# A streaming prefix log-sum-exp: straight-line programs with rising semaphores in place of token loops, and a different last tile

## The chip, the cores and the metric

One core of one Trainium2 chip runs the kernel. The metric is device microseconds of one execution on that core.

## The reference

The input is 8 x 4096 x 2048 in float32 (268 MB), and so is the output. Along the middle axis each output row is the logarithm of the sum of exponentials of all rows so far:

```python
out[:, 0, :] = x[:, 0, :]
for t in range(1, S):
    mx = np.maximum(out[:, t - 1, :], x[:, t, :])
    out[:, t, :] = mx + np.log(np.exp(out[:, t - 1, :] - mx) + np.exp(x[:, t, :] - mx))
```

## The kernel before

The kernel works on 64 tiles of 4 MB: 128 partitions with 4 successive rows of 2048 columns each, so that a partition's part is 32 KB in one piece, in memory and on the chip. Six tile buffers turn round. For each tile, ScalarE takes the exponential in two column halves; VectorE sums the 4 rows of each partition (`local`); TensorE multiplies the partition totals by a triangle of ones, which gives what lies before each partition (`triangle`); VectorE adds it (`join`); TensorE carries the last partition's total to the next tile (`carry`); ScalarE takes the logarithm, and issues the store. SyncE issues the loads.

Three of the engines run loops of six tiles. So that a loop's turns can all wait for the same numbers, each wait is a token: it waits for a count and takes it off again.

```python
def take(engine, s, n):
    event(engine, [(s, n)], [(s, "sem-sub-imm", n)])
...
@block.sync                       # loads
    sp.dma_start(out=ti[0][:, 0:2, :], in_=x_v[0][:, 0:2, :]).then_inc(top, 16)
    sp.dma_start(out=ti[0][:, 2:R, :], in_=x_v[0][:, 2:R, :]).then_inc(loaded[0], 16)
    ...
    with sp.Fori(1, turns + 1) as j:
        for n in range(NI):
            take(sp, stored[n], 16)
            load(x_v[bass.ds(j * NI + n, 1)][0], n)
    ...
    for n in range(NT - NI, NT):  # last waits, inside the block
        take(sp, stored[n % NI], 32 if n >= NT - 2 else 16)
...
@block.scalar                     # its end: tiles 62 and 63 leave in column halves
    exp(n, 0)
    if n < NT - 1:
        exp(n, 1)
    ln(up, 0, turn)
    if n == NT - 1:
        store(up, o_v[up], turn, 0)
        exp(n, 1)
    ln(up, 1, turn)
    store(up, o_v[up], turn, 1 if n == NT - 1 else None)
    ...
    for h in range(2):
        ln(NT - 1, h, NT - 1 - first)
        store(NT - 1, o_v[NT - 1], NT - 1 - first, h)
    settle(NT - first)            # takes the tokens of a turn off
```

The softmax here doesn't subtract the row's maximum and nothing guards it: scores larger than these inputs give would overflow.

## Time and profile before

| | before |
|---|---|
| time, median of the first 3 runs | 1250.83 us (1250.73 to 1252.3) |
| bytes read and written | 537 MB |
| mean rate over the span | 430 GB/s |
| instructions in the record | 3456 |
| busy share of VectorE / ScalarE | 82% / 73% |

The page's DMA row says in tenths how busy the 16 DMA engines are in each of 40 slices, the row under it how much they moved. In the groups, the last column says how long the engine stood idle before such an instruction and what ended that. The prediction below shows the main lines. Two more lines of the page, the packets and the second instruction queue, are needed later:

```profile
DMA packets 20409, 537.01 MB, mean 430 GB/s; under 512 B 2096, under 2 KB 2096, under 8 KB 4144
...
q14 instruction: 2, 0.02, 0.0%
```

Packets under 8 KB are the semaphore writes (2096) and the 2048 packets of 4 KB in which the last two tiles leave. And the first transfer, in the order of time (start, duration):

```profile
1.03 0.39 SPq L114 DMA_DIRECT2D ti<-in_x_dram  x1
```

### The profile page before, as it was taken

What the parts mean: (1) busy time and instruction counts of PE and PEld (TensorE: products, weight loads), DVE (VectorE), ACT (ScalarE), POOL (GpSimd) and SP (SyncE); (2) the same over time, 40 slices, a digit from 0 to 9 for tenths busy, and PEclk for the clock granted to TensorE, in tenths of its full rate; (3) what the DMA queues carried; (4) which work ended last, traced back from release to release, by engine and by line L of the source; (5) the groups of instructions that cost most, each with busy time, mean ns of one, the idle gap of its engine ahead of it and who ended that gap; (6) DMA issues with size and microseconds to landing.
All of it is one profiled execution on the core that took longest, in us unless ns stands there. A gap on an engine that the chain in (4) does not pass through costs nothing. (4 is left out here: it accounts for less than half of the span.)

```text
span 1249.0 us, 3456 instructions
## 1 busy us (share of the span) xinstructions
PE 650.8 (52%) x960; PEld 215.3 (17%) x960; DVE 1023.0 (82%) x512; ACT 907.2 (73%) x258; POOL 1.1 (0%) x8
## 2 busy tenths in 40 slices
PE   3556455554566545655455544565545564465541
PEld 1112111111112111211111111121111121111110
DVE  4999978778787787887878878778787787877873
ACT  5897866867768677686776866867768677686774
POOL 0000000000000000000000000000000000000000
PEclk9897778786887868778778786777878878678785
DMA  9999999999999999999999999999999999999998
GB/s 403 420 436 430 433 430 437 433 431 434 430 436 434 431 433 430 437 434 430 434 430 436 436 430 434 430 436 437 428 434 431 436 436 429 434 430 436 436 430 354
DMA packets 20409, 537.01 MB, mean 430 GB/s; under 512 B 2096, under 2 KB 2096, under 8 KB 4144
## 3 DMA queue, kind: packets, MB, share of 16 engines
q1 hardware_dynamic: 9360, 268.44, 49.9%
q10 hardware_dynamic: 11040, 268.44, 49.9%
q8 instruction: 7, 0.11, 0.0%
q14 instruction: 2, 0.02, 0.0%
HBM read 268.44 MB, written 268.44 MB: 430 GB/s over the span
## 5 line engine op out<-in xcount | busy, mean ns | idle before, releaser
L136 ACT ACTIVATE ti<-ti 128x4096 f32<-128x4096 f32 (+1 forms) x128 | 452.6, 3582 | 310.2 <-ACTq L59 304.2
L232 DVE TENSOR_TENSOR ti<-ti 128x1024 f32<-128x1024 f32 x384 | 464.7, 1224 | 200.0 <-ACT ti L136 191.3
L241 DVE TENSOR_TENSOR ti<-ti,ps 128x4096 f32<-128x4096 f32 x128 | 560.0, 4416 | 9.4 <-PE ps L208 9.0
L208 PE MATMUL ps<-ti,before 128*128 128x512 f32 x512 | 380.4, 895 | 342.6 <-DVE ti L232 342.1
L142 ACT ACTIVATE ti<-ti 128x4096 f32<-128x4096 f32 x128 | 455.4, 3602 | 11.5 <-PE ps L197 6.0
L197 PE MATMUL ps<-ti,last 128*128 128x512 f32 x448 | 270.6, 735 | 234.2 <-DVE ti L241 234.2
L208 PEld LDWEIGHTS ps<-ti,before 128*128 128x128 f32 x512 | 128.7, 279 | 609.0 <-DVE ti L232 500.9
L197 PEld LDWEIGHTS ps<-ti,last 128*128 128x128 f32 x448 | 86.6, 214 | 401.8 <-DVE ti L241 334.7
L159 ACT ACTIVATE ti<-ti 128x4096 f32<-128x4096 f32 x1 | 3.6, 3616 | 6.5 <-ACTq L59 6.5
L32 ACT ACT_TABLE_LOAD x1 | 1.3, 1283 | 0.8 <-PEq L274 0.8
L103 POOL TENSOR_SCALAR_AFFINE_SELECT last<-last 128x128 f32<-128x128 f32 x1 | 0.3, 296 | 0.0
L98 POOL TENSOR_SCALAR_AFFINE_SELECT before<-before 128x128 f32<-128x128 f32 x1 | 0.3, 295 | 0.1
L95 POOL MEMSET last<- 128x128 f32 x1 | 0.2, 206 | 0.0
L94 POOL MEMSET before<- 128x128 f32 x1 | 0.2, 205 | 0.5 <-SPq L77 0.5
L274 POOL MEMSET const-bfloat16-1.0<- 128x1 bf16 x1 | 0.1, 103 | 0.0
L274 POOL MEMSET const-uint8-127<- 128x1 uint8 x1 | 0.1, 103 | 0.0
L274 POOL MEMSET const-float32-0.0<- 128x1 f32 x1 | 0.1, 99 | 0.3 <-issue 0.3
L274 POOL MEMSET const-float32-1.0<- 128x1 f32 x1 | 0.1, 99 | 0.0
## 6 DMA issues: line engine op xcount, KB each, us to landing
ti<-in_x_dram SPq DMA_DIRECT2D x63, 4096.0 KB, 38.4
out_dram<-ti ACTq DMA_DIRECT2D x62, 4096.0 KB, 44.0
out_dram<-ti ACTq DMA_DIRECT2D x4, 2048.0 KB, 12.9
ti<-in_x_dram SPq DMA_DIRECT2D x2, 2048.0 KB, 9.7
```

What stands on the lines that cost most here:

```text
L32: nc.scalar.preload_act_table_set("natural_log_exp_and_others")
L94: g.memset(before[:], 1.0).then_inc(ones, 1)
L98: g.affine_select(out=before[:], in_=before[:], compare_op=mybir.AluOpType.is_ge, fill=0.0, base=-1, pattern=[[1, P]], channel_multiplier= ...
L103: g.affine_select(out=last[:], in_=last[:], compare_op=mybir.AluOpType.is_ge, fill=0.0, base=-(P - 1), pattern=[[0, P]], channel_multiplier=1,
L136: act.activation(t[:, rows, half(h)], t[:, rows, half(h)], ACT.Exp).then_inc(exps[h], 1)
L142: act.activation(t[:, :, half(h)], t[:, :, half(h)], ACT.Ln)._wait_ge(carried[h], turn + 1).then_inc(logs, 1)
L159: act.activation(ti[0][:, 0:2, :], ti[0][:, 0:2, :], ACT.Exp)
L197: m = pe.matmul(ps[(n + 1) % 2][:, sl], last[:], ti[n % NI][:, R - 1, sl], start=True, stop=False, skip_group_check=True,)
L208: m = pe.matmul(ps[n % 2][:, sl], before[:], ti[n % NI][:, R - 1, sl], start=n % NBLK == 0, stop=True, skip_group_check=True,)
L232: a = dve.tensor_add(t[:, r, half(h)], t[:, r - 1, half(h)], t[:, r, half(h)])
L241: dve.tensor_add(t[:, :, half(h)], t[:, :, half(h)], ps[n % 2][:, half(h)].unsqueeze(1).to_broadcast([P, R, HALF]),)._wait_ge(ahead[h], n ...
L274: nc = _bacc.Bacc("TRN2", target_bir_lowering=False, num_devices=1)
```

## The change

The intent: no loops, so no register work, no tokens, no taking off at a turn's end, and waits that ride on the instruction that needs them; the last tile in long runs of memory rather than short ones; and first loads and last waits beside the block and its barrier. The core of the diff:

```diff
+    class Count:
+        def __init__(self, name):
+            self.s, self.n = tc.alloc_semaphore(name), 0
+        def __call__(self, inst, by=1):
+            inst.then_inc(self.s, by)
+            self.n += by
+            return self.n
...
+        for rows, c in ((slice(0, 2), top), (slice(2, R), loaded[0])):
+            c(nc.sync.dma_start(out=ti[0][:, rows, :], in_=x_v[0][:, rows, :]), 16)
         with nc.Block() as block:
...
             @block.sync
             def _(sp):
-                with sp.Fori(1, turns + 1) as j:
-                    for n in range(NI):
-                        take(sp, stored[n], 16)
-                        load(x_v[bass.ds(j * NI + n, 1)][0], n)
-                (and first loads, last loads, last waits)
+                for n in range(1, NT):
+                    i = n % NI
+                    if n >= NI:
+                        sp.wait_ge(stored[i].s, n // NI * 16)
+                    loaded[i](sp.dma_start(out=ti[i][:], in_=x_v[n]), 16)
...
             @block.scalar
-                (loop, settle, column halves of tiles 62 and 63)
+                def ln(n):
+                    t = ti[n % NI]
+                    for h in range(2):
+                        for rows in parts(n) if h else [slice(0, R)]:   # two row halves for the last tile
+                            logs(act.activation(
+                                t[:, rows, half[h]], t[:, rows, half[h]], ACT.Ln
+                            )._wait_ge(carried[h].s, n + 1))
+                            if h:
+                                act.wait_ge(logs.s, logs.n)
+                                stored[n % NI](act.dma_start(
+                                    out=o_v[n][:, rows, :], in_=t[:, rows, :]
+                                ), 16)
+                exp(0)
+                for n in range(NT):
+                    if n + 1 < NT:
+                        exp(n + 1)
+                    ln(n)
...
+        for c in stored:
+            nc.sync.wait_ge(c.s, c.n)
```

VectorE's and TensorE's work is the same, in the same order, without the loop and the takes.

More of the change, by code (lines that the diff above doesn't have):

```diff
@@ L36 @@
     R = 4
+    NI = 6
+    FD = 512
+    HALF = D // 2
     NBLK = S // (P * R)
     NT = B * NBLK
-    FD = 512
-    NI = 6
-    HALF = D // 2
-    assert NI % 2 == 0 and NBLK % 2 == 0 and D == 4 * FD
+    assert D == 4 * FD
     pool = ctx.enter_context(tc.tile_pool(name="io", bufs=1))
@@ L52 @@
     o_v = out.rearrange("b (k p r) d -> (b k) p r d", p=P, r=R)
-    def half(h):
-        return slice(h * HALF, (h + 1) * HALF)
-    def event(engine, waits, updates):
-        engine.add_instruction(mybir.InstEventSemaphore(
-            name=f"I-{nc.next_id()}", engine=engine.engine, ins=[], outs=[],
-            sync_info=mybir.SyncInfo(
-                on_wait=[mybir.SyncWait(
-                    sync_type="semaphore", id=s.num, ant_name=s.name,
-                    wait_mode="sem-ge-imm", wait_value=n,
-                ) for s, n in waits],
-                on_update=[mybir.SyncUpdate(
-                    sync_type="semaphore", id=s.num, ant_name=s.name,
-                    update_mode=mode, update_value=n,
-                ) for s, mode, n in updates],
-            ),
-        ))
@@ L73, in take, with parts @@
-    def take(engine, s, n):
-        event(engine, [(s, n)], [(s, "sem-sub-imm", n)])
+    half = [slice(h * HALF, (h + 1) * HALF) for h in range(2)]
+    def parts(n):
+        m = 2 if n == NT - 1 else 1
+        return [slice(k * R // m, (k + 1) * R // m) for k in range(m)]
+    class Count:
[5 more added lines that the diff above has]
+            return self.n
@@ L77, with counts @@
     with tc.tile_critical():
-        def sems(name, n):
-            return [nc.alloc_semaphore(f"{name}{i}") for i in range(n)]
-        ones, shaped, logs, top = (
-            sems(s, 1)[0] for s in ("ones", "shaped", "logs", "top")
-        )
-        loaded, stored = sems("loaded", NI), sems("stored", NI)
-        exps, chain, sums, ahead, joined, carried = (
-            sems(s, 2) for s in ("exps", "chain", "sums", "ahead", "joined", "carried")
-        )
+        def counts(name, n):
+            return [Count(f"{name}{i}") for i in range(n)]
@@ L90 @@
+        ones, shaped, logs, top, chain = (
+            Count(s) for s in ("ones", "shaped", "logs", "top", "chain")
+        )
+        loaded, stored = counts("loaded", NI), counts("stored", NI)
+        exps, sums, ahead, joined, carried = (
+            counts(s, 2) for s in ("exps", "sums", "ahead", "joined", "carried")
+        )
+        for rows, c in ((slice(0, 2), top), (slice(2, R), loaded[0])):
+            c(nc.sync.dma_start(out=ti[0][:, rows, :], in_=x_v[0][:, rows, :]), 16)
         with nc.Block() as block:
@@ L93, in _ @@
             def _(g):
-                g.memset(before[:], 1.0).then_inc(ones, 1)
-                g.memset(last[:], 1.0).then_inc(ones, 1)
-                g.wait_ge(ones, 2)
-                g.affine_select(
+                ones(g.memset(before[:], 1.0))
+                ones(g.memset(last[:], 1.0))
+                g.wait_ge(ones.s, ones.n)
+                shaped(g.affine_select(
                     out=before[:], in_=before[:], compare_op=mybir.AluOpType.is_ge, fill=0.0,
                     base=-1, pattern=[[1, P]], channel_multiplier=-1,
-                ).then_inc(shaped, 1)
@@ L103, in _ @@
-                g.affine_select(
+                ))
+                shaped(g.affine_select(
                     out=last[:], in_=last[:], compare_op=mybir.AluOpType.is_ge, fill=0.0,
                     base=-(P - 1), pattern=[[0, P]], channel_multiplier=1,
-                ).then_inc(shaped, 1)
+                ))
             @block.sync
             def _(sp):
-                def load(src, n):
-                    sp.dma_start(out=ti[n][:], in_=src).then_inc(loaded[n], 16)
-                sp.dma_start(out=ti[0][:, 0:2, :], in_=x_v[0][:, 0:2, :]).then_inc(top, 16)
@@ L115, in _ @@
-                sp.dma_start(out=ti[0][:, 2:R, :], in_=x_v[0][:, 2:R, :]).then_inc(loaded[0], 16)
-                for n in range(1, NI):
-                    load(x_v[n], n)
-                turns = (NT - NI) // NI
-                with sp.Fori(1, turns + 1) as j:
-                    for n in range(NI):
-                        take(sp, stored[n], 16)
-                        load(x_v[bass.ds(j * NI + n, 1)][0], n)
-                for n in range((turns + 1) * NI, NT):
-                    take(sp, stored[n % NI], 16)
-                    load(x_v[n], n % NI)
@@ L126, in _, with exp @@
-                for n in range(NT - NI, NT):
-                    take(sp, stored[n % NI], 32 if n >= NT - 2 else 16)
+                for n in range(1, NT):
[3 more added lines that the diff above has]
+                    loaded[i](sp.dma_start(out=ti[i][:], in_=x_v[n]), 16)
             @block.scalar
             def _(act):
-                def exp(n, h, rows=slice(0, R)):
+                def exp(n):
                     t = ti[n % NI]
-                    if h == 0:
-                        take(act, loaded[n % NI], 16)
-                    act.activation(
-                        t[:, rows, half(h)], t[:, rows, half(h)], ACT.Exp
-                    ).then_inc(exps[h], 1)
@@ L140, in ln @@
-                def ln(n, h, turn):
-                    t = ti[n % NI]
-                    act.activation(
-                        t[:, :, half(h)], t[:, :, half(h)], ACT.Ln
-                    )._wait_ge(carried[h], turn + 1).then_inc(logs, 1)
-                def store(n, dst, turn, h=None):
-                    cols = slice(0, D) if h is None else half(h)
-                    act.wait_ge(logs, 2 * turn + (2 if h is None else h + 1))
-                    act.dma_start(
-                        out=dst[:, :, cols], in_=ti[n % NI][:, :, cols]
-                    ).then_inc(stored[n % NI], 16)
@@ L153, in settle @@
-                def settle(turns):
-                    take(act, carried[0], turns)
-                    take(act, carried[1], turns)
-                    take(act, logs, 2 * turns)
-                take(act, top, 16)
-                act.activation(ti[0][:, 0:2, :], ti[0][:, 0:2, :], ACT.Exp)
-                exp(0, 0, slice(2, R))
-                exp(0, 1, slice(2, R))
-                turns = (NT - 2) // NI
-                with act.Fori(0, turns) as j:
-                    for n in range(1, NI + 1):
-                        exp(n, 0)
-                        exp(n, 1)
-                        ln(n - 1, 0, n - 1)
-                        ln(n - 1, 1, n - 1)
-                        store(n - 1, o_v[bass.ds(j * NI + (n - 1), 1)][0], n - 1)
-                    settle(NI)
@@ L171, in _ @@
-                first = turns * NI
-                for n in range(first + 1, NT):
-                    up, turn = n - 1, n - 1 - first
-                    exp(n, 0)
-                    if n < NT - 1:
-                        exp(n, 1)
-                    ln(up, 0, turn)
-                    if n == NT - 1:
-                        store(up, o_v[up], turn, 0)
-                        exp(n, 1)
-                    ln(up, 1, turn)
-                    store(up, o_v[up], turn, 1 if n == NT - 1 else None)
@@ L183, in _ @@
-                for h in range(2):
-                    ln(NT - 1, h, NT - 1 - first)
-                    store(NT - 1, o_v[NT - 1], NT - 1 - first, h)
-                settle(NT - first)
+                    lo = 0
+                    if n == 0:
+                        lo = 2
+                        act.activation(t[:, :lo], t[:, :lo], ACT.Exp)._wait_ge(top.s, 16)
+                    for h in range(2):
+                        a = act.activation(t[:, lo:, half[h]], t[:, lo:, half[h]], ACT.Exp)
+                        if h == 0:
+                            a._wait_ge(loaded[n % NI].s, (n // NI + 1) * 16)
+                        exps[h](a)
@@ new lines, in ln @@
+                def ln(n):
+                    t = ti[n % NI]
+                    for h in range(2):
+                        for rows in parts(n) if h else [slice(0, R)]:
[7 more added lines that the diff above has]
+                                ), 16)
@@ L192, in carry @@
                     if n % NBLK == NBLK - 1:
-                        event(pe, [(joined[h], n + 1)], [(carried[h], "sem-add-imm", 1)])
+                        pe.wait_ge(joined[h].s, n + 1)
+                        pe.sem_inc(carried[h].s, 1)
                         return
@@ L201, in carry @@
                         if c == 2 * h:
-                            m._wait_ge(joined[h], n + 1)
-                    m.then_inc(carried[h], 1)
+                            m._wait_ge(joined[h].s, n + 1)
+                    carried[h](m)
                 def triangle(n, h):
@@ L212, in triangle @@
                         if c == 2 * h:
-                            m._wait_ge(sums[h], n + 1)
-                    m.then_inc(ahead[h], 1)
-                pe.wait_ge(shaped, 2)
+                            m._wait_ge(sums[h].s, n + 1)
+                    ahead[h](m)
+                pe.wait_ge(shaped.s, shaped.n)
                 for n in range(NT):
@@ L222, in _ @@
                         carry(n, h)
-                for h in range(2):
-                    take(pe, sums[h], NT)
-                    take(pe, joined[h], NT)
             @block.vector
@@ L229, in local @@
                 def local(n, h):
-                    t = ti[n]
+                    t, cols = ti[n % NI], half[h]
                     for r in range(1, R):
-                        a = dve.tensor_add(t[:, r, half(h)], t[:, r - 1, half(h)], t[:, r, half(h)])
+                        a = dve.tensor_add(t[:, r, cols], t[:, r - 1, cols], t[:, r, cols])
                         if r == 1:
-                            a._wait_ge(exps[h], n + 1)
+                            a._wait_ge(exps[h].s, n + 1)
                         else:
-                            a._wait_ge(chain[h], (R - 2) * n + r - 1)
-                        a.then_inc(*((chain[h], 1) if r < R - 1 else (sums[h], 1)))
+                            a._wait_ge(chain.s, chain.n)
+                        (chain if r < R - 1 else sums[h])(a)
                 def join(n, h):
-                    t = ti[n]
-                    dve.tensor_add(
-                        t[:, :, half(h)], t[:, :, half(h)],
-                        ps[n % 2][:, half(h)].unsqueeze(1).to_broadcast([P, R, HALF]),
-                    )._wait_ge(ahead[h], n + 1).then_inc(joined[h], 1)
-                def turn(tiles):
-                    for n in range(tiles):
-                        for h in range(2):
-                            local(n, h)
-                        for h in range(2):
-                            join(n, h)
-                    for h in range(2):
-                        take(dve, exps[h], tiles)
-                        take(dve, chain[h], (R - 2) * tiles)
-                        take(dve, ahead[h], tiles)
-                with dve.Fori(0, NT // NI):
-                    turn(NI)
-                turn(NT % NI)
+                    t, cols = ti[n % NI], half[h]
+                    joined[h](dve.tensor_add(
+                        t[:, :, cols], t[:, :, cols],
+                        ps[n % 2][:, cols].unsqueeze(1).to_broadcast([P, R, HALF]),
+                    )._wait_ge(ahead[h].s, n + 1))
+                for n in range(NT):
+                    for h in range(2):
+                        local(n, h)
+                    for h in range(2):
+                        join(n, h)
+        for c in stored:
+            nc.sync.wait_ge(c.s, c.n)
 _INS = ['x']
```

## The prediction

> **What bounds the kernel now.** I read the page first (busy shares, the DMA row, the queues, the groups), then the same stretches of the run as a table by stage, then the order of work on the scalar engine in the last 40 us, then the records of DMA packets and of semaphore landings in the trace.
>
> ```profile
> PE 650.8 (52%) x960; PEld 215.3 (17%) x960; DVE 1023.0 (82%) x512; ACT 907.2 (73%) x258; POOL 1.1 (0%) x8
> ...
> DMA  9999999999999999999999999999999999999998
> GB/s 403 420 436 430 433 430 437 433 431 434 430 436 434 431 433 430 437 434 430 434 430 436 436 430 434 430 436 437 428 434 431 436 436 429 434 430 436 436 430 354
> ...
> q8 instruction: 7, 0.11, 0.0%
> ...
> HBM read 268.44 MB, written 268.44 MB: 430 GB/s over the span
> ...
> L136 ACT ACTIVATE ti<-ti 128x4096 f32<-128x4096 f32 (+1 forms) x128 | 452.6, 3582 | 310.2 <-ACTq L59 304.2
> ...
> ti<-in_x_dram SPq DMA_DIRECT2D x63, 4096.0 KB, 38.4
> out_dram<-ti ACTq DMA_DIRECT2D x62, 4096.0 KB, 44.0
> ```
>
> No compute engine is full: 82% of VectorE and 73% of ScalarE. The DMA row is full in every slice but the last, at 430 to 437 GB/s. ScalarE is idle for 310 us before its Exp, of which 304.2 us end at a token wait (L59): the wait for a loaded tile. So data movement sets the pace. The 537 MB are the input read once and the output written once; the change moves the same bytes.
>
> The table by stage (columns: window, its length, busy of PE, PEld, DVE, ACT, POOL with counts, granted clock, DMA share, GB/s):
>
> ```profile
> 0.00:2.00 2.00, 0.00 (x0) 0.00 (x0) 0.00 (x0) 1.19 (x1) 1.09 (x8) 1.00 0.00 0
> 2.00:62.00 60.00, 28.05 (x44) 9.17 (x44) 45.92 (x24) 42.01 (x14) 0.00 (x0) 0.91 1.01 428
> 62.00:1200.00 1138.00, 608.45 (x896) 201.40 (x896) 952.12 (x479) 839.25 (x239) 0.00 (x0) 0.78 1.00 433
> 1200.00:1224.00 24.00, 10.69 (x18) 3.75 (x18) 16.50 (x10) 17.48 (x5) 0.00 (x0) 0.86 0.99 429
> 1224.00:1244.00 20.00, 3.59 (x4) 0.98 (x4) 8.41 (x2) 7.23 (x2) 0.00 (x0) 0.50 1.00 410
> 1244.00:1249.00 5.00, 0.00 (x0) 0.00 (x0) 0.00 (x0) 0.00 (x0) 0.00 (x0) 0.50 0.11 47
> ```
>
> What is left to win is plain from it: 2 us before the first byte, a loss of 5% in the 20 us of 1224 to 1244 (410 against 433, so some 1 us), and 5 us at the end with nearly nothing moving. Everything else runs at the full rate.
>
> The packet records say why the end is ragged. A 32 KB packet (one partition of a tile) takes 1213 ns on its DMA engine; 1024 of them per engine are 1242.1 us, and the slowest engine runs from 2.04 (first packet) to 1247.66 (last landing), 1245.6 us. Of the 16 landings of the last store the first is at 1243.71, the median at 1244.7, the 15th at 1245.47 and the last alone at 1247.66: one engine is 2.2 us behind the rest, and has been falling behind slowly since about 500 us (some 0.04 us per tile). The time is therefore that one engine's queue, never empty, plus start and end.
>
> [...] The trace shows 7 fetches of 16,384 B in queue q8, about 160 us apart, which fits TensorE's straight program (256 instructions at some 31 per tile are 8.3 tiles of 19.4 us), each 0.88 to 0.97 us long. [...] the trace's loop branches take 40 to 62 ns in the sequencers.
>
> **The change, part by part.**
>
> (a) *Loops and tokens go.* ScalarE has 98 token events, VectorE 66, the DMA-issuing SyncE 64, TensorE 20, at 17 to 51 ns: about 5.2 us of sequencer time in 1249. With them go the turn ends (9 or 10 per engine, a register op and a branch, some 0.1 us each) and the two register ops (46 + 29 ns) before each dynamic transfer. Are they on the path? A tile's slot is taken for six tile periods, 6 x 19.37 = 116 us. The load takes 38.4 us from issue to landing and the store 44.0, while one load and one store sharing the engines need 19.4 us each: so 38.4 - 19.4 + 44.0 - 19.4 = 43.6 us of queueing. A compute chain that is shorter by 0.2 us per tile only lengthens that queue. Gain: 0.0 us.
>
> (b) *Longer programs.* ScalarE gets about 129 Exp, 129 Ln, 65 waits, 65 stores, some 390 instructions; VectorE 512; SyncE about 125. Against the looped programs (my estimate: 130, 100 and 60) that is some 730 instructions more, 47 KB [...], or 3 blocks. Each holds one DMA engine some 0.6 us (16 KB at the 609 to 613 ns that 16 KB packets of the first loads take). If one or none of them falls to the slowest engine: +0.2 us on average, 0 to 1.2.
>
> (c) *First loads ahead of the block.* The trace has the entry barrier done at 0.7, a NOP at 0.8, the block's branch at 0.9 and the first load issued at 1.03, its first packet at 2.04. Without the branch it should be issued near 0.88: -0.15 us, and all of it counts, as the engines are never empty afterwards.
>
> (d) *Last two tiles.* Before, tiles 62 and 63 leave as four column halves in 4 KB packets (2048 packets; their median is 159 ns, eight of them 1272 ns against 1213). On the slowest engine the landings of these four are 1232.87, 1237.82, 1242.73, 1247.66 after 1227.90: 19.76 us. The change sends tile 62 whole (9.73 us, as tile 61 took from 1218.17 to 1227.90) and tile 63 in row halves of 16 KB packets (2 x 4.88, as the two halves of the first load landed at 8.51 and 13.39): 19.49. So -0.27 us.
>
> (e) *Last waits outside the block.* After the last landing at 1247.66 come the block's drain and barrier (1247.7 to 1247.9), the critical section's (1248.0 to 1248.2) and the context's two barriers and semaphore clear (to 1249.0). The first is passed early now: -0.25 us. Clearing more semaphores should stay in the one range clear, 0.07 us.
>
> Sum: 0.0 + 0.2 - 0.15 - 0.27 - 0.25 = -0.47, so 1250.83 - 0.47 = 1250.36. I say **1250.3**.
>
> **Rivals.**
>
> *The last stores come too late.* Before, the engine order at the end is:
>
> ```profile
> 1208.53 3.62 ACT L136 ACTIVATE ti<-ti 128x4096 f32<-128x4096 f32 x1 [5.29 <-ACTq L59]
> 1212.05 3.60 ACT L142 ACTIVATE ti<-ti 128x4096 f32<-128x4096 f32 x1
> 1215.68 0.63 ACTq L149 DMA_DIRECT2D out_dram<-ti  x1
> 1216.36 3.62 ACT L136 ACTIVATE ti<-ti 128x4096 f32<-128x4096 f32 x1 [0.71 <-ACT ti L142]
> 1219.88 3.60 ACT L142 ACTIVATE ti<-ti 128x4096 f32<-128x4096 f32 x1
> 1223.51 0.54 ACTq L149 DMA_DIRECT2D out_dram<-ti  x1
> ...
> 1231.86 0.54 ACTq L149 DMA_DIRECT2D out_dram<-ti  x1
> ...
> 1236.18 0.54 ACTq L149 DMA_DIRECT2D out_dram<-ti  x1
> ```
>
> The reader is to see that half of tile 62 leaves at 1215.68. With the change four activations of 3.6 us come first: 1208.5 + 14.3 = 1222.9 for all of tile 62, first packet 1.0 us later (as with the first load), 1223.9. Store 61 has landed on the fastest engine at 1223.69, on the median one at 1224.86, on the slowest at 1227.90. So the fastest may idle 0.2 us, and the one that counts has 4 us in hand. Tile 63: VectorE starts its second half at 1215.9 in place of 1220.0, joins end at 1224.1 and 1228.4, its carry some 0.1 later; Ln of the left half to 1227.8, of the upper right 1228.5 to 1230.4 (1.86 us, the Exp of that shape), issue near 1230.5 and 1233.0, against 1231.9 and 1236.2 before. The slowest engine needs them at 1237.6 and 1242.5. So nothing starves. If I am wrong by 4 us, it costs up to 4 us: 1254.
>
> *Tokens are on the path after all.* Then at most their 5.2 us and 2 us of turns come back: 1244. The DMA share of 1.00 from 62 to 1200 speaks against it.
>
> *Fetches hurt more.* Three blocks all on the slowest engine[...]: +2 us, 1252. [...] only bytes on the slowest engine count.
>
> **Range and chances.** The parts that I trust sum to -0.7 and the fetches span 0 to +1.2. The runs of before themselves lie from 1250.73 to 1252.3, and the lag of the one slow engine can shift by half a microsecond. Range 1248.8 to 1252.0. A change of 2% is 25 us; all time in which the DMA engines aren't full is some 8 us, so faster by 2% is out of reach (0.005), and slower needs a new stall in each tile (0.01). Within 2%: 0.985.
>
> **What would show it.** DMA full again from slice 1 to 39 and 433 GB/s in the middle; ScalarE's idle time before Exp again about 300 us, now with the load itself as releaser; first load issued before 0.95; no packets of 2 to 8 KB; more than 7 instruction packets; tile 62's store issued near 1223 and the last near 1233, with 10 us and more of draining after it; less than 1.2 us from the last landing to the end. Wrong would be shown by a drop of the rate between 1215 and 1230 (late stores), by a load and a store taking other than 19.4 us a tile, or by one engine's lag grown by more than 1 us.

Three things are cut from the recorded text, at the marks: what it told of the hardware from outside this case, where it took the 64 bytes of an instruction in (b) from, and the stall of an engine in a rival. The 47 KB of (b) stand on the trace of the kernel before: between the starts of the first and the last of the seven fetches of 16,384 bytes, at 106.53 and 1087.90 us, TensorE starts 1534 instructions (matmuls, weight loads and semaphore events), and 6 x 16,384 / 1534 = 64 bytes each (1526 and 64 in the changed kernel). The some 730 instructions, the author's estimate, are then 47 KB, or 3 blocks of that size.

## The result and the profile after

| | before | after |
|---|---|---|
| median of 5 runs each | 1251.26 us (1250.73 to 1252.3) | 1250.73 us (1250.54 to 1252.27) |
| profiled span | 1249.0 us | 1248.8 us |
| instructions in the record | 3456 | 2916 |
| last landing of a store, in the trace | 1247.66 us | 1246.77 us |
| from there to the end of the span | 1.37 us | 2.06 us |

The ratio is 0.9997 with a 95% interval of 0.9983 to 1.0012: the same time. (A ratio is the mean time of one kernel's runs over that of the other's in the same rounds, so it is not quite the ratio of the medians.) A difference under some 2 us cannot be had from these times. (A landing is a semaphore update by which a transfer reports that a share of it is done: in the kernel before 2096 for 131 transfers, 16 each, and a transfer is done with the last. They are read here as one for each of the 16 DMA engines. In the kernel before the trace has 16 to 18 packets in work each microsecond from 1218.5 to 1242.5, and a single one at 1245.5 and 1246.5, between the 15th landing of the last store (1245.47) and the last (1247.66), at a DMA share of 0.06 (one of 16) from 1245 to 1247; so what lands last is called one late engine.)

The page of the changed kernel, lines that answer to those of before:

```profile
span 1248.8 us, 2916 instructions
...
GB/s 403 420 431 431 430 437 436 427 434 432 437 435 426 435 432 437 433 428 435 431 437 433 430 435 430 437 431 432 436 430 436 432 432 435 431 436 432 431 435 361
DMA packets 18735, 537.06 MB, mean 430 GB/s; under 512 B 2080, under 2 KB 2080, under 8 KB 2080
...
q14 instruction: 8, 0.07, 0.0%
...
L121 ACT ACTIVATE ti<-ti 128x4096 f32<-128x4096 f32 (+1 forms) x128 | 452.5, 3582 | 308.2 <-DMA ti<-in_x_dram 306.0
```

ScalarE still stands idle for 308 us before its Exp. What ends it is now named as the load itself (306.0 us), since the wait rides on the activation, but it is the same wait. The packets of 4 KB are gone (2080 under 8 KB are semaphore writes), and six more blocks of instructions of 8 KB each were fetched in q14.

The table by stage (same columns as in the prediction), the stages that can differ:

```profile
62.00:1200.00 1138.00, 603.83 (x897) 199.82 (x898) 952.05 (x480) 838.57 (x238) 0.00 (x0) 0.79 1.00 433
1200.00:1224.00 24.00, 12.38 (x20) 3.91 (x18) 20.34 (x10) 17.10 (x6) 0.00 (x0) 0.79 1.00 432
1224.00:1244.00 20.00, 0.00 (x0) 0.00 (x0) 3.92 (x1) 7.15 (x3) 0.00 (x0) 0.56 0.97 418
1244.00:1249.00 5.00, 0.00 (x0) 0.00 (x0) 0.00 (x0) 0.00 (x0) 0.00 (x0) 0.50 0.10 41
```

The middle is at 433 GB/s as before. From 1224 to 1244 the rate is 418 in place of 410. And the start and end in the order of time:

```profile
1.02 0.85 SPq L84 DMA_DIRECT2D ti<-in_x_dram  x2
```

```profile
1207.90 7.12 ACT L121 ACTIVATE ti<-ti 128x4096 f32<-128x4096 f32 x2 [5.23 <-DMA ti<-in_x_dram]
1214.93 7.11 ACT L130 ACTIVATE ti<-ti 128x4096 f32<-128x4096 f32 x2
1222.07 0.34 ACTq L135 DMA_DIRECT2D out_dram<-ti  x1
...
1229.98 0.34 ACTq L135 DMA_DIRECT2D out_dram<-ti  x1
...
1232.31 0.34 ACTq L135 DMA_DIRECT2D out_dram<-ti  x1
```

The first load is issued where it was: 1.02 against 1.03 us, and the first packet starts at 2.04 in both traces. Tile 62 is issued at 1222.07 and the halves of tile 63 at 1229.98 and 1232.31, each within a microsecond of the times worked out in the prediction, and the engines do not run empty for it.

### The profile page after: what moved, and what is told of

Same layout as the page of the kernel before. It is cut to its first block, busy times and chain, and to the rows that moved or that the text cites. A ratio compares the mean times of both kernels' runs of the same rounds, so it can differ in the third digit from the quotient of the medians.

```text
span 1248.8 us, 2916 instructions
## 1 busy us (share of the span) xinstructions
PE 645.1 (52%) x960; PEld 213.4 (17%) x960; DVE 1022.3 (82%) x512; ACT 907.5 (73%) x259; POOL 1.1 (0%) x8
## 2 busy tenths in 40 slices
DMA packets 18735, 537.06 MB, mean 430 GB/s; under 512 B 2080, under 2 KB 2080, under 8 KB 2080
## 4 chain that ended last, share of the span: by engine, by line
DMA 80%; ACT 14%; DVE 4%; PE 1%; DVEq 0%; issue 0%; SPq 0%; ACTq 0%; PEldq 0%
DMA out_dram<-ti 41%; DMA ti<-in_x_dram 38%; ACT ti L130 7%; ACT ti L121 7%; DVE ti L195 2%; DVE ti L186 1%; PE ps L166 1%; DVEq L86 0%; PE ps L155 0%; SPq L84 0%; ACTq L135 0%; PEldq L151 0%; SPq L233 0%; SPq L69 0%
## 5 line engine op out<-in xcount | busy, mean ns | idle before, releaser
L121 ACT ACTIVATE ti<-ti 128x4096 f32<-128x4096 f32 (+1 forms) x128 | 452.5, 3582 | 308.2 <-DMA ti<-in_x_dram 306.0
L186 DVE TENSOR_TENSOR ti<-ti 128x1024 f32<-128x1024 f32 x384 | 464.6, 1224 | 196.6 <-ACT ti L121 187.9
L166 PE MATMUL ps<-ti,before 128*128 128x512 f32 x512 | 373.2, 879 | 347.1 <-DVE ti L186 347.0
## 6 DMA issues: line engine op xcount, KB each, us to landing
ti<-in_x_dram SPq DMA_DIRECT2D x63, 4096.0 KB, 38.5
```

Source lines behind the costliest of these rows:

```text
L121: a = act.activation(t[:, lo:, half[h]], t[:, lo:, half[h]], ACT.Exp)
L166: m = pe.matmul(ps[n % 2][:, sl], before[:], ti[n % NI][:, R - 1, sl], start=n % NBLK == 0, stop=True, skip_group_check=True,)
L186: a = dve.tensor_add(t[:, r, cols], t[:, r - 1, cols], t[:, r, cols])
```

## The experiments

Twelve kernels. The ratios below are against the kernel before, run in the same rounds (its medians there are 1250.81 to 1250.95 us), also where the edit was made to the changed kernel. The theory: the DMA engines' bytes set the pace, everything that was removed lay in the shadow of them, and what is left are fractions of a microsecond at the two ends. The rivals: sequencers and tokens are on the path after all; or the compute chain has no slack; or the fetches of longer programs cost what the tokens gave.

### Is it the bytes? Half of each store left out

```diff
-                                    out=o_v[n][:, rows, :], in_=t[:, rows, :]
+                                    out=o_v[n][:, 0:2, :], in_=t[:, 0:2, :]
```

(and no row halves for the last tile; half of the output is not written, so the result is wrong)

> The changed kernel storing only 2 of the 4 rows per partition of each tile (wrong result on purpose: half of the output is not written). Bytes fall to 3/4, 14.5 us a tile for the DMA engines. Theory (bytes set the pace, VectorE comes next with 7.40 + 8.72 = 16.1 us a tile): 64 x 16.1 + 15 at the start + some 20 at the end = 1067 us (1050 to 1090), VectorE over 93% busy. If sequencers or waits set the pace, little change from 1251.

Measured: 1057.62 us, ratio 0.8453 (0.8436 to 0.847), within the span given. The page's busy line:

```profile
PE 571.1 (54%) x960; PEld 188.0 (18%) x960; DVE 1015.3 (96%) x512; ACT 915.1 (87%) x258; POOL 1.1 (0%) x8
```

VectorE is now busy for 96% of the span, with the same instructions as before. Taking bytes away shortens the kernel by 193 us, to the next bound; so the bytes are the present one.

### Is there room on ScalarE? One activation more per tile, and two

```diff
+                    if n:
+                        for e, r in zip(extra, [4]):        # second kernel: [4, 3]
+                            act.activation(
+                                e[:], before[:].unsqueeze(1).to_broadcast([P, r * 8, P]), ACT.Exp
+                            )._wait_ge(shaped.s, 2)
                     for h in range(2):
                         a = act.activation(t[:, lo:, half[h]], t[:, lo:, half[h]], ACT.Exp)
```

> The changed kernel with one more activation of 128x4096 per tile (into a tile that nobody reads): ScalarE does 14.2 + 3.6 = 17.8 us a tile, under 19.4. Theory (DMA engines set the pace): unchanged, 1250.7 within 2 us, ScalarE's idle time before the Exp falls by some 220 us. Rival (ScalarE's order of work is on the path): up to + 63 x 3.6 = 227 us.

Measured: 1250.62 us (1250.56 to 1251.22), ratio 1.0 (0.9983 to 1.0016). The group of the Exp:

```profile
L127 ACT ACTIVATE ti<-ti 128x4096 f32<-128x4096 f32 (+1 forms) x128 | 452.3, 3580 | 63.9 <-DMA ti<-in_x_dram 63.8
```

Its idle time fell from 308 to 64 us: 227 us of more work went into the gap, and the time did not move.

> As before but a second more activation of 128x3072 per tile, 2.7 us: ScalarE does 20.5 us a tile, over 19.4, and becomes the bound: 63 x 20.5 + some 35 us of start and end = 1325 us (1305 to 1345), ScalarE over 95% busy, DMA share down to about 0.94.

Measured: 1348.15 us, ratio 1.0778 (1.0757 to 1.08), ScalarE busy for 96%. The kind is right and the size was 23 us short, 3 us outside the span given: the extra activations kept ScalarE busy for 395 us, as foretold (63 x 6.3 = 397), but it was idle for another 26 us before them. One more thing is seen here. From 200 to 600 us the DMA share is 0.99, where 0.94 was expected, while the rate is 408 GB/s:

```profile
200.00:600.00 400.00, 199.87 (x296) 65.69 (x295) 310.55 (x156) 391.69 (x117) 0.00 (x0) 0.75 0.99 408
```

So a DMA share near 1.00 does not prove that the engines are at their limit. The mean record of a 32 KB packet in this stretch is 1267 ns, against 1213 in the kernel after, with the median unchanged at 1213. The rate is the better witness.

### Is there slack in the chain? Four buffers, and three

```diff
-    NI = 6
+    NI = 4        # second kernel: 3
```

> The changed kernel with 4 tile buffers in place of 6. Theory (a slot's 116 us hold 43.6 us of mere queueing, so the compute chain has slack): least slot time is 19.4 (load beside a store) + 33.8 (116.2 - 38.4 - 44.0, landing to store issue) + 19.4 (store) = 72.6 us, under 4 x 19.37 = 77.5, so the time stays at 1250.7, within 2 us; load and store times to landing fall to a sum of about 44. Rival (the latencies are real service times): 116.2 / 4 = 29 us a tile, 1860 us.

Measured: 1292.44 us (1283.87 to 1294.82), ratio 1.031 (1.0274 to 1.0346). The expectation was wrong by 42 us; the rival's 1860 was wrong by far more. The transfers (last column: median us from issue to landing):

```profile
ti<-in_x_dram SPq DMA_DIRECT2D x63, 4096.0 KB, 23.1
out_dram<-ti ACTq DMA_DIRECT2D x63, 4096.0 KB, 22.8
```

Load and store fell from 38.5 and 44.0 to 23.1 and 22.8. Their sum, 45.9, is close to the 44 that was foretold, but the estimate of the least slot time had used 19.4 for each. With 33.8 us for the chain between them, a slot takes 79.7 us, and 79.7 / 4 = 19.9 us a tile against 19.37: 64 x 0.55 = 35 us, most of the 42 measured. So the slack of the six-buffer kernel is 116.2 - 79.7 = 36 us and not 43.6, which is still many times what the tokens could take.

> The changed kernel with 3 tile buffers. Theory: 72.6 us no longer fit into 3 x 19.37 = 58.1, so the DMA engines run empty and the time rises; with transfers that speed up when the other direction pauses (9.7 + 1 us each) the least slot time is 55.2, so somewhere between 1260 and 1560, my estimate 1340. If it stays at 1251, the chain is shorter than I read it.

Measured: 1489.25 us, ratio 1.1906 (1.1882 to 1.193). Within the span given, above its estimate: load 15.9, store 16.4, so the slot keeps (1489 / 64) x 3 = 69.8 us, of which 37.5 are not transfers.

### Run length magnified: every store in 4 KB runs

```diff
-                                stored[n % NI](act.dma_start(
-                                    out=o_v[n][:, rows, :], in_=t[:, rows, :]
-                                ), 16)
+                                for cols in half:
+                                    stored[n % NI](act.dma_start(
+                                        out=o_v[n][:, :, cols], in_=t[:, :, cols]
+                                    ), 16)
```

(with the loads waiting for 32 per tile, and no row halves)

> The changed kernel with every tile stored as two column halves, both issued where the one store was, so that all stores go in 4 KB packets (part (d) of the change magnified 32 times in the opposite sense). By the landings of the last tiles of the kernel before (19.76 against 19.46 us for two tiles): 0.15 us a tile, + 9.6 us, 1260. By the packets' own times (8 x 159 against 1213 ns): 0.47 us a tile, + 30 us, 1281. Rival (run length does not matter where the engines are full): 1251.

Measured: 1288.59 us (1287.68 to 1289.07), ratio 1.0301 (1.0283 to 1.0318). The time rose by 37.6 us, for 64 tiles 0.59 us each. That is more than the packets' own times give (0.47), and four times what the last tiles of the kernel before, which had no load beside them, gave (0.15). The page shows two more effects, in the transfers, and in the chain that ended last and ScalarE's waits:

```profile
out_dram<-ti ACTq DMA_DIRECT2D x128, 2048.0 KB, 34.5
ti<-in_x_dram SPq DMA_DIRECT2D x63, 4096.0 KB, 16.6
...
ACT 66%; ACTq 26%; DVE 4%; DMA 1%; PE 1%; issue 1%; DVEq 0%; SPq 0%; PEldq 0%
...
L121 ACT ACTIVATE ti<-ti 128x4096 f32<-128x4096 f32 (+1 forms) x128 | 452.5, 3582 | 354.0 <-issue 346.7
```

Loads now land after 16.6 us in place of 38.5, and the mean record of a load's packet from 200 to 600 us rose from 1213.4 to 1237.0 ns. And ScalarE no longer waits for loads: it is held in its own store issues (ACTq). By the trace the 128 of them take 342 us in all, up to 15.2 us each, where the 65 of the changed kernel take 22 us; the chain that ended last lies 92% on ScalarE, where it lay 80% on transfers. So this edit also filled ScalarE, and the 37.6 us are not shown to be the run length's alone. Whether the short packets at the DMA engines, or the held issues, or both, set this time was not taken apart.

### The tail alone

The kernel before, with tile 62 whole and tile 63 in row halves; loops and tokens stay.

```diff
                     exp(n, 0)
-                    if n < NT - 1:
-                        exp(n, 1)
+                    exp(n, 1)
                     ln(up, 0, turn)
-                    if n == NT - 1:
-                        store(up, o_v[up], turn, 0)
-                        exp(n, 1)
                     ln(up, 1, turn)
-                    store(up, o_v[up], turn, 1 if n == NT - 1 else None)
-                for h in range(2):
-                    ln(NT - 1, h, NT - 1 - first)
-                    store(NT - 1, o_v[NT - 1], NT - 1 - first, h)
+                    store(up, o_v[up], turn)
+                (left half whole, right half and store by rows 0:2 and 2:4)
```

> The kernel before with part (d) alone: loops and tokens stay, tile 62 leaves whole and tile 63 in two row halves. Theory: the last two tiles take 19.45 us on the slowest engine in place of 19.76, so - 0.3 us (1250.9), and the time from the last landing to the end stays at 1.4 us as in the kernel before, where the changed kernel needs 2.06. In the trace: no packets of 2 to 8 KB, two instruction packets in q14. The timing will hardly tell 0.3 us from noise.

Measured: 1250.47 us (1250.28 to 1250.75), ratio 0.9994 (0.9981 to 1.0008), not to be told from before. In the trace the slowest engine's landings go from 1217.98 (store of tile 60) to 1247.18, 29.20 us for three tiles, against 1218.17 to 1247.66, 29.49, in the kernel before: -0.29. The last landing is 1.37 us before the end, as in the kernel before. This is the lowest median among the kernels with the right result, but it isn't shown to be faster than either kernel.

### The last waits back in the block

```diff
                     loaded[i](sp.dma_start(out=ti[i][:], in_=x_v[n]), 16)
+                for n in range(NT - NI, NT):
+                    k = n // NI * 16 + (32 if n == NT - 1 else 16)
+                    sp.wait_ge(stored[n % NI].s, k)
...
-        for c in stored:
-            nc.sync.wait_ge(c.s, c.n)
```

> The changed kernel with the final waits back inside the block of SyncE, in order of the tiles, so that the last store is waited for last. By the prediction's step (e) this costs 0.25 us (block barrier after the last landing). By what the trace of the changed kernel shows (three more waits, 0.20 us, and a branch, 0.15 us, after the last landing) it costs some - 0.1 us. The time from the last landing to the end tells: 2.3 us for the prediction, 1.9 to 2.0 for the trace reading; 2.06 now.

Measured: 1250.53 us (1250.48 to 1250.87), ratio 0.9994 (0.9981 to 1.0008); last landing to the end 2.15 us. Neither number given: taking the waits out of the block is worth 0.09 us (this one trace against five straight-line ones at 2.06), and both of these kernels take some 0.7 us longer to end than the looped ones, whose five traces all show 1.37. In the trace of the changed kernel, that 0.7 consists of a branch that SyncE takes after its last wait (0.15), two more wait instructions after the one for the last store (0.12, since the waits go by buffer number and not by tile), a stop ahead of a NOP of SyncE (0.41 in place of 0.04), and a semaphore clear of 0.22 in place of 0.07, less the block's barrier (0.25) and some smaller steps. The stop is there with the waits in the block as well, and not in the longer straight-line kernel below, which ends in 1.63 us. What causes it was not found.

### Tokens magnified

The kernel before, with 20 pairs of token events more per tile in both transfer-issuing loops.

```diff
+        def tokens(engine, s):
+            for _ in range(20):
+                event(engine, [], [(s, "sem-add-imm", 1)])
+                take(engine, s, 1)
...
+                        tokens(sp, extra[1])
                         take(sp, stored[n], 16)
...
+                        tokens(act, extra[0])
                         exp(n, 0)
```

> The kernel before with 20 more token pairs (add one, take one) per tile in the loops of ScalarE and SyncE: 40 events at some 55 ns pitch are 2.2 us of sequencer time per tile, some 130 us on each engine, 25 times what the change removed. Theory (tokens are hidden): 1251 within 2 us. Rival (tokens are on the path): up to 1380.

Measured: 1260.56 us (1259.47 to 1261.58), ratio 1.0077 (1.006 to 1.0093). Neither theory: the added events (2400 on ScalarE, 2160 on SyncE) fill 173 us of ScalarE's sequencer and 132 us of SyncE's by the trace, 72 and 61 ns each where the 55 were an estimate, and that did not go onto the path, but 9.6 us did appear. The record holds 4541 instructions more. The landings say where it went: the first of 16 landings of each tile keeps its pace (1204.4 us for the load of tile 63, as in the kernel before), and the last comes at 1217.6 in place of 1208.4. One DMA engine falls behind: 11.1 us after the 15th landing of that load, where the kernel before shows 1.4.

### Satisfied waits as straight-line code

```diff
                     i = n % NI
+                    for _ in range(40):
+                        sp.wait_ge(top.s, 16)
...
                 for n in range(NT):
+                    for _ in range(40):
+                        act.wait_ge(top.s, 16)
```

> The changed kernel with 40 satisfied waits more per tile on ScalarE and SyncE: the same sequencer time as the token test, but as straight-line code, 2 x 2520 instructions, some 320 KB or 40 fetches of 8 KB in queue q14, each 0.31 us on one DMA engine. Theory (b): spread over 16 engines + 0.8 us, all on the slowest + 12; I expect + 1 to + 6 us, 1252 to 1257. Rival (a wait's sequencer time counts): 1380.

(The 320 KB are 5040 instructions at the 64 bytes that the trace of the kernel before shows for TensorE.)

Measured: 1261.19 us (1260.85 to 1261.31), ratio 1.0079 (1.0063 to 1.0096). Again not 1380, but more than the span given. The compiler put two waits into one instruction, so the record holds 2540 more than that of the changed kernel, not 5040. So this is not the same sequencer time as in the token loop, but about half: 91 us on ScalarE and 68 on SyncE. And there were 19 more fetches than in the changed kernel's 8, not 40 (2540 x 64 bytes are 163 KB, or 20 fetches of 8 KB):

```profile
q14 instruction: 27, 0.22, 0.0%
```

At 0.31 us each that is 5.9 us at most, if all fell on one engine, against 10.2 us. So fetches are not enough, and in the token loop there were only 4 more of them. Here two engines are late: for the load of tile 63 the last landing is 12.7 us after the median one and the 15th 5.4 us, where the changed kernel shows 1.7 for both. Something that goes with instructions seems to cost a DMA engine time; the next test asks for that.

### Instructions on an engine that has no part in the work

The kernel before, with GpSimd looping over satisfied waits beside the scan (the second kernel: 504 turns).

```diff
+                g.wait_ge(shaped, 2)
+                with g.Fori(0, 252):
+                    for _ in range(40):
+                        g.wait_ge(ones, 2)
```

> The kernel before, with GpSimd, which has no part in the scan after its two masks, running a loop of satisfied waits beside it: 252 turns, 20 wait instructions each (two waits go into one), 5040 instructions, some 0.06 us each, so from 2 us to about 320 us. It issues no transfer and delays none. Theory A (every instruction that any engine runs costs one DMA engine a little time, 9.6 us / 4541 = 2.1 ns by the token loop): + 10 us, to 1261, with one engine's landings falling behind the others until about 320 us and no longer. Theory B (the token loop and the long waits lost their 10 us because they held up the issue of transfers on SyncE and ScalarE): 1251, no lag beyond the 2.2 us of the kernel before.

Measured: 1256.87 us (1256.68 to 1256.95), ratio 1.0042 (1.0024 to 1.006).

> The same with 504 turns, 10080 instructions, to about 640 us. Theory A: + 20 us, to 1271, the lag growing to 640 us. Theory B: 1251.

Measured: 1263.15 us (1263.11 to 1263.42), ratio 1.0093 (1.0075 to 1.0111).

Theory B falls: GpSimd issues nothing and holds up nothing, and the time rises by 6.0 and 12.2 us. Theory A's size was too large by a factor of two. The records grew by 5545 and 11089 instructions, so 6.0 / 5545 = 1.07 and 12.2 / 11089 = 1.10 ns an instruction: proportional. The loops ran until 491 and 981 us (0.087 us an instruction, not the 0.06 foretold), and the lag of the last landing behind the 15th grows fast while they run and slowly after: in the shorter loop 5.8 us at 528 us and 7.1 at 935; in the longer one 6.4 at 528, 13.0 at 935 and 14.0 at 1109. Its rate row shows when the bill is paid:

```profile
GB/s 399 422 433 433 432 434 431 435 432 432 432 432 431 432 432 431 433 434 433 433 433 432 432 433 434 432 433 433 431 432 432 432 432 432 432 434 434 434 355 274
```

From the third slice on it stays at 431 to 435, and the last two slices fall to 355 and 274. From 1224 to 1244 us the DMA share is 0.66 at 271 GB/s, where the kernel before has 1.00 at 410. With the lag of the last landing this is read as engines that have finished their share of the loads and wait while one works off its backlog.

What it is about an instruction that costs the engine 1.1 ns was not shown. Nor does that figure alone explain the other two tests. The token loop cost 2.1 ns an instruction (9.6 / 4541). Each of its instructions also changes a semaphore, which the satisfied waits do not: its trace holds 4558 more semaphore changes than that of the kernel before, the longer GpSimd loop 3 more. At 1.1 ns the instructions make 5.0 us, and the other 4.6 would be 1.0 ns a change, an estimate that no run tests. For the long waits, 2540 instructions at 1.1 ns (2.8 us) and all fetches on one engine (5.9) make 8.7 of the 10.2 us at most.

## Why the prediction was right

The time fell inside the range and the forecast of no change within 2% held. By its own steps:

- *The bound.* Right: without half of the stores 1057.6, with 227 us more of ScalarE unchanged. Its argument from the DMA share was weaker than it sounded, as the share stays at 0.99 at 408 GB/s with two extra activations.
- *(a) Loops and tokens, 0.0.* Right in its main point: some twenty times as many tokens were hidden as sequencer time. The slack was 36 us, not 43.6, because a load and a store took 45.9 us together in the four-buffer kernel, and not 38.8. It missed that the number of instructions has a price outside their own engine. For the 540 instructions that the change removes, 1.1 ns each are an estimate of 0.6 us. The traces agree in sign: up to the landing of the store of tile 59 the changed kernel's slowest engine is 0.56 us ahead (1208.07 against 1208.63), and its last landing there is 1.72 us after the median one, against 3.25; the tail alone, with its loops, still has 3.15, and the straight-line kernel with the waits in the block 2.37. (Behind the 15th landing it is 0.01 us, but only because two engines are equally late there.) One trace each, with fetches mixed in, so this is argued more than shown. The lag of the kernel before grew faster than the prediction read: behind the 15th landing from 0.01 us at 509 us to 2.24 at 1209, some 0.06 us a tile, not 0.04.
- *(b) Longer programs, +0.2.* The size in bytes was right (47 KB foretold, 6 x 8 KB measured: 8 fetches in q14 against 2). The time was not isolated; each of the six takes 0.31 us on one engine, where (b) reckoned with some 0.6 for a block of 16 KB.
- *(c) First loads ahead of the block, -0.15.* Wrong: 0.0, and its sign (first load before 0.95 us) failed at 1.02. The branch that was taken for the block's stands ahead of the first load in the changed kernel too (0.86 us, then the load at 1.02), so it isn't the block's, and entering a block costs the issue nothing here.
- *(d) Last two tiles, -0.27.* Right: -0.31 us in the changed kernel (1227.32 to 1246.77 is 19.45 us against 19.76), -0.32 in the tail alone (1227.74 to 1247.18). Nothing starved: 16 packets or more were in work at each microsecond from 1222 to 1242. (The prediction's own Ln times put the second half's store near 1232.3, not 1233.0; it came at 1232.31.)
- *(e) Last waits outside the block, -0.25.* Wrong in sign for the whole end: 1.37 us became 2.06, where less than 1.2 was the sign named, and the semaphore clear took 0.22 us, not 0.07. The step itself is worth -0.09; the straight-line program with its other semaphores ends more slowly.

So in the two traces: -0.58 until the store of tile 61 has landed, -0.31 for the last two tiles, +0.69 after the last landing, in sum -0.20 us, where -0.47 was foretold. Steps (c) and (e) failed by 0.15 and 0.94, and what was gained before the tail made up for most of it. A total that came near from partly wrong terms is luck, and the times, which cannot tell less than 2 us apart, do not confirm it. What was not luck is the forecast of no visible change: all time in which the engines aren't full is some 8 us of 1250.

## What to carry to other kernels

Where bytes set the pace, first add up how much time there is at all in which the DMA engines move less than their full rate; here 8 us, so no rewrite of loops and waits could gain 1%. Then ask of a removed wait what it waits for: one that ends with the arrival of data cost nothing on its own engine here (of the token loop's 173 us on ScalarE's sequencer, the time showed 9.6, with one DMA engine late); what instructions cost was 1.07 to 2.1 ns each on a late DMA engine. And read the rate rather than the DMA share, and the landing times engine by engine rather than as a median: here one late engine out of 16 set the end of each large transfer (2.2 us behind the 15th landing at the end of the kernel before, 14.0 us at 1109 us in the longer GpSimd loop).
